# Gate/up blocks of a hybrid decoder layer: the first four pairs product by product on the unscaled residual stream

## The chip, the cores and the metric

The kernel runs on one core of a Trainium2 chip. The metric is the device time of one execution in microseconds (us). Weights and activations lie in device memory as float32 and reach the core's on-chip buffer by DMA; TensorE multiplies, its results land in PSUM banks of 512 float32 per partition, and VectorE, ScalarE and GpSimd do the rest.

## What is computed

One decoder block over 16 meta tokens and 512 tokens of width 1024: two token mixers (mLSTM and gated linear attention) side by side, then a SwiGLU channel mixer with 2816 hidden features and a final norm. The part that matters here, cut from the reference:

```python
def rmsnorm(x, g):
    y = xf * lax.rsqrt(jnp.mean(xf * xf, axis=-1, keepdims=True) + EPS)
    return (y * g.astype(jnp.float32)).astype(x.dtype)
...
    h = h + merged @ w_out[l].astype(dt)

    hn = rmsnorm(h, norm2_g[l])
    ff = jax.nn.silu(hn @ w_ff_gate[l].astype(dt)) * (hn @ w_ff_up[l].astype(dt))
    h = h + ff @ w_ff_down[l].astype(dt)

out = rmsnorm(h, final_g)
```

## The kernel before

Activations are kept transposed: features on the 128 partitions, the 512 tokens along a row. Each operand is split into a high part (a rounded copy, made by ScalarE) and a low part (the remainder, made by VectorE), and each product is three matmuls: high x high, high x low, low x high. For weights the copy is `whi` (line 215) and the remainder `wlo` (line 220); a unit of weights is 128x1024, loaded by SyncE into `raw` some units ahead.

Most products are done in pairs of feature blocks (`pair`, `seven`): the product of a 2x2 blocked operand by seven products of half the width instead of eight, called q1, q5, q6, p2, p3, p4 and p7. A pair has three PSUM banks (`bz`, `bx`, `by`). Some products add into the bank that an earlier one filled, after a copy of the earlier value has been taken out. A *sink* names what is done with the banks: copies s1, s7, s2 by ScalarE (lines 1641, 1642), additions c21, c11, c22 by VectorE (1643 to 1645), and `mid`, `c12`, `fin`. The weights of a pair are the gate and up rows, their sums (`wf`, line 254, and `wg`, line 266) and the splits of all of these; half of the sums come from DMAs that add to what is in the buffer.

In time the kernel goes through the projections, the two mixers, the branch products ("bm", "bg"), four pairs for the output projection ("out"), the feed-forward blocks, and the down product. The order in which an engine gets its work is the order in which the program writes it. Generators hold the side work; each product step advances them (`tick`), and `yield n` in one of them puts off its next piece by n steps. Tables (`PLAIN`, `FIRST`, `SECOND`, `DOWN`) say at which step of a unit the next units' weights are split.

After the out pairs, `residual` puts each block of h into `hres` and makes plain high and low operands `hf` of h times the norm's gain (lines 1494, 1495). The first four feature blocks (`NSTD`) are done plainly: `unit_real` (lines 335 to 337) does each gate and each up block as 8 x 3 matmuls of 512 columns on `hf`. Meanwhile `norm2` computes the row factor `rs2` (1 over the root mean square, one number per token), `operands` builds the seven operands for the pairs from h times gain times `rs2` (lines 1595 to 1616, splits 1586 and 1588), and `swiglu` multiplies gate and up by `rs2` (1552, 1553), takes Silu on ScalarE and forms their product on GpSimd (1557). The other 18 pairs follow: `sink_ff` applies Silu (line 144) and multiplies the halves (1637).

The down product goes through its seven products one after the other over all 11 pairs of hidden blocks; the results are added to `hres` (line 1740). Its last product, p3, is done output group by output group, 0, 1, 2, 3; groups 0 and 1 lie in one PSUM bank, 2 and 3 in another (`out_of`). Sums of down weights are formed ahead of time in device memory (`down_sums`, one step at each `next(sums)`) by GpSimd's and SyncE's DMA queues.

## Time and profile before

| | |
|---|---|
| median of 3 runs | 911.99 us (910.56 to 912.91) |
| profiled execution | 911.17 us |
| span in its trace | 909.4 us |
| TensorE busy | 894.3 us, 98% |
| VectorE / ScalarE / GpSimd busy | 707.0 / 582.5 / 129.0 us (78, 64, 14%) |
| out pairs, plain units | about 486 to 560 us, 560 to 606 us |
| 18 gate/up pairs, down product | 606 to 788 us, 788 to 900 us |

The span runs from the first to the last instruction that the profiler saw. Matmuls overlap in the records: one lasts longer than the time until the next one starts, so a pace is read from starts.

### The profile page before, as it was taken

What the parts mean: (1) busy time and instruction counts of PE and PEld (TensorE: products, weight loads), DVE (VectorE), ACT (ScalarE), POOL (GpSimd) and SP (SyncE); (2) the same over time, 40 slices, a digit from 0 to 9 for tenths busy, and PEclk for the clock granted to TensorE, in tenths of its full rate; (3) what the DMA queues carried; (4) which work ended last, traced back from release to release, by engine and by line L of the source; (5) the groups of instructions that cost most, each with busy time, mean ns of one, the idle gap of its engine ahead of it and who ended that gap; (6) DMA issues with size and microseconds to landing.
All of it is one profiled execution on the core that took longest, in us unless ns stands there. A gap on an engine that the chain in (4) does not pass through costs nothing. (4 is left out here: it accounts for less than half of the span.)

```text
span 909.4 us, 17138 instructions
## 1 busy us (share of the span) xinstructions
PE 894.3 (98%) x6615; PEld 852.4 (94%) x6615; DVE 707.0 (78%) x1144; ACT 582.5 (64%) x1062; POOL 129.0 (14%) x151
## 2 busy tenths in 40 slices
PE   9999999999999999999999999999999999999995
PEld 9998989899998899999997898879999999999995
DVE  4789676888865477787778988897767767889995
ACT  6578578898774275766774455645555555667673
POOL 0000022021211122222110112133112111000000
PEclk9999999999999999999999999999999999999998
DMA  9346274569885889888874788269777776475652
GB/s 339 135 159 181 84 188 89 144 185 243 208 221 171 213 227 246 218 210 187 175 166 128 191 223 209 70 157 207 182 202 173 191 202 155 116 221 175 192 146 93
DMA packets 73538, 164.22 MB, mean 181 GB/s; under 512 B 7184, under 2 KB 24720, under 8 KB 72112
## 3 DMA queue, kind: packets, MB, share of 16 engines
q1 hardware_dynamic: 50208, 125.20, 41.5%
q0 software_dynamic: 22016, 36.84, 26.1%
q10 hardware_dynamic: 1232, 1.09, 0.4%
q8 instruction: 51, 0.84, 0.4%
q14 instruction: 31, 0.25, 0.1%
HBM read 156.68 MB, written 28.44 MB: 204 GB/s over the span
## 5 line engine op out<-in xcount | busy, mean ns | idle before, releaser
L381 PE MATMUL b<-t,whi 128*128 128x256 f32 (+1 forms) x1008 | 288.8, 286 | 3.1 <-DVE t L1516 1.1
L383 PE MATMUL b<-t,wlo 128*128 128x256 f32 (+1 forms) x1008 | 284.4, 282 | 0.3 <-DVE wlo L220 0.3
L382 PE MATMUL b<-t,whi 128*128 128x256 f32 (+1 forms) x1008 | 284.6, 282 | 0.0
L220 DVE TENSOR_TENSOR wlo<-raw,whi 128x1024 fp32r<-128x1024 f32 (+2 forms) x175 | 209.1, 1196 | 91.0 <-ACT whi L215 90.7
L215 ACT CAST whi<-raw 128x1024 fp32r<-128x1024 f32 (+2 forms) x175 | 178.8, 1023 | 59.9 <-PE b L382 21.8
L381 PEld LDWEIGHTS b<-t,whi 128*128 128x128 f32 x1008 | 190.0, 188 | 4.8 <-DVE t L1516 1.5
L382 PEld LDWEIGHTS b<-t,whi 128*128 128x128 f32 x1008 | 190.1, 189 | 0.5
L383 PEld LDWEIGHTS b<-t,wlo 128*128 128x128 f32 x1008 | 189.9, 188 | 0.5 <-DVE wlo L220 0.5
L336 PE MATMUL b<-t,whi 128*128 128x264 f32 (+1 forms) x528 | 178.6, 338 | 0.2 <-DVE t L972 0.2
L335 PE MATMUL b<-t,whi 128*128 128x264 f32 (+1 forms) x480 | 162.2, 338 | 0.0
L337 PE MATMUL b<-t,wlo 128*128 128x264 f32 (+1 forms) x480 | 159.6, 332 | 0.0
L144 ACT ACTIVATE t<-t 128x512 f32<-128x512 f32 (+8 forms) x145 | 80.6, 573 | 53.2 <-DVE t L1316 22.8
L1793 PE MATMUL b<-t,whi 128*128 128x256 f32 x616 | 110.5, 282 | 1.0 <-DVE f L1740 1.0
L336 PEld LDWEIGHTS b<-t,whi 128*128 128x128 f32 x528 | 99.9, 189 | 11.8 <-DVE t L972 0.8
L335 PEld LDWEIGHTS b<-t,whi 128*128 128x128 f32 x480 | 91.1, 190 | 8.9 <-ACT t L967 0.3
L337 PEld LDWEIGHTS b<-t,wlo 128*128 128x128 f32 x480 | 90.8, 189 | 8.7
L1793 PEld LDWEIGHTS b<-t,whi 128*128 128x128 f32 x616 | 95.1, 189 | 1.4 <-DVE f L1740 1.4
L198 POOL DMA_DIRECT2D raw<-wst x42 | 37.0, 882 | 385.6 <-DMA raw<-wst 68.1
L1793 PE MATMUL b<-t,wlo 128*128 128x256 f32 x308 | 86.8, 282 | 0.0
L1793 PEld LDWEIGHTS b<-t,wlo 128*128 128x128 f32 x308 | 58.3, 189 | 0.0
L239 POOL DMA_DIRECT2D wf<-wst x42 | 41.3, 991 | 115.7 <-ACT t L144 33.4
L215 ACT CAST whi<-wf 128x1024 fp32r<-128x1024 f32 x42 | 44.0, 1048 | 19.9 <-PE b L382 11.6
(273 smaller groups left out, 1469.3 us busy)
## 6 DMA issues: line engine op xcount, KB each, us to landing
raw<-wst SPq DMA_DIRECT2D x131, 512.0 KB, 4.9
wf<-wst SPq DMA_DIRECT2D x42, 256.0 KB, 4.2
wf<-wst POOLq DMA_DIRECT2D x42, 256.0 KB, 6.4
raw<-wst POOLq DMA_DIRECT2D x42, 256.0 KB, 4.5
raw<-wdn SPq DMA_DIRECT2D x15, 512.0 KB, 3.7
sum_q<-wdn POOLq DMA_DIRECT2D x10, 512.0 KB, 9.3
raw<-sum_q SPq DMA_DIRECT2D x10, 512.0 KB, 3.6
sum_q<-wdn SPq DMA_DIRECT2D x5, 512.0 KB, 5.3
```

What stands on the lines that cost most here:

```text
L144: S.activation(o, i, func, **kw)
L198: G.dma_start(lr(r, 0), lr(wst[v - 1], 0), accum_op=ALU.add)
L215: S.copy(t, src)
L220: V.tensor_tensor(t, src, hi.bitcast(F32), ALU.subtract)
L239: G.dma_start(lr(st.f, 1), lr(wst[u + 1], 1), accum_op=ALU.add)
L335: T.matmul(o, w_h, ah[:, c0:c1], start=first, stop=False)
L336: T.matmul(o, w_h, al[:, c0:c1], start=False, stop=False)
L337: T.matmul(o, w_l, ah[:, c0:c1], start=False, stop=last)
L381: T.matmul(o, h, xh_[k][:, c0:c1], start=start and k == 0, stop=False, skip_group_check=not start)
L382: T.matmul(o, h, xl_[k][:, c0:c1], start=False, stop=False, skip_group_check=not start)
L383: T.matmul(o, l, xh_[k][:, c0:c1], start=False, stop=k == 3, skip_group_check=not start)
L1793: T.matmul(o, w[ws][:, j * P:(j + 1) * P], xd[n][k][:, xs_], start=fresh and step == 0, stop=step == 2 and k == FH - 1, skip_group_check=True)
```

## The change

The four plain blocks become one *group* of four gate and four up blocks that goes through the seven products one after the other, as the down product does: 14 chunks (`GCHUNKS`, 7 products by two halves of the inner dimension) of 24 matmuls with 256 columns. Their weights are sums formed ahead of time in device memory (`gsum`, from the new input `wgu`). The operands are h times gain without the row factor. They are built from `residual`'s copies during the out pairs, and `norm2` runs inside the group. Since gate and up would both need the row factor, only the gate is multiplied by it, ahead of Silu; the residual `hres` is divided by the factor once (the final norm doesn't see a factor of the row, but for its eps, which `done` adds in), so that ff and residual have the same scale. In `sink_ff` this puts a multiply (`gate`) ahead of each Silu. The product of `swiglu` on GpSimd is gone; VectorE does it in the group. Also: the groups of p3 run in the order 0, 2, 1, 3; the residual's loads (`load_x`) start in the "bg" units; one pair's weight sum is made by VectorE (`e_hi`); some `yield` numbers differ.

```diff
+LAST = (0, 2, 1, 3)
+GCHUNKS = [(n, k) for n in ORDER for k in (0, 2)]
 CHUNKS = [(n, 0, k, min(2, FH - k)) for n in ORDER[:-1] for k in range(0, FH, 2)] + [
-    ("p3", i, k, n) for i in range(4) for k, n in ((0, 6), (6, 5))]
+    ("p3", i, k, n) for i in LAST for k, n in ((0, 6), (6, 5))]
...
     def e_hi(u):
+        if u == FF0:
+            r = lr(raws[u + 1], 0)
+            V.tensor_tensor(r, r, lr(raws[u], 0), ALU.add)
         mixw[u].eh = whi(raws[u + 1])
...
-        if what in ("bm", "bg") and i % 2 or len(job) == 2:
+        if what in ("bm", "bg") and i % 2 or len(job) == 2 or job in JOBS[3:8]:
             next(sums, None)
...
-            if i == 3:
-                load_x(0)
+            if i in (1, 2, 5, 6):
+                load_x(2 * (1, 5, 2, 6).index(i))
...
     def residual(m, t):
         hres.append(t)
-        g = pr[:, C_N2 + m:C_N2 + m + 1]
-        a, b = tt(F32R, NS), tt(F32R, NS)
-        act(a, t, AF.Copy, scale=g)
-        V.scalar_tensor_tensor(b, t, g, a.bitcast(F32), ALU.mult, ALU.subtract)
-        hf[0].append(a)
-        hf[1].append(b)
...
+        act(hx[m // 2][:, m % 2], t, AF.Copy, scale=pr[:, C_N2 + m:C_N2 + m + 1])
+        full[0] = m + 1
+        yield 3
+        yield from add_square(m, t)
...
+        V.scalar_tensor_tensor(r, x, -2.0, y, ALU.mult, ALU.mult)
+        nbank.v = None
+        yield 42
+        for m in range(8):
+            yield 9
+            V.tensor_tensor(hres[m], hres[m], r, ALU.mult)
...
-        t1, t2 = tt(n=NS), tt(n=NS)
-        V.tensor_tensor(t1, og, rs2.v, ALU.mult)
-        V.scalar_tensor_tensor(t2, ou, -1.0, rs2.v, ALU.mult, ALU.mult)
-        yield 2
-        act(t1, t1, AF.Silu)
-        yield 5
-        G.tensor_tensor(t2, t1, t2, ALU.mult)
...
+            def gate(c, src):
+                V.tensor_tensor(g[:, c], src, rs2.v[:, c], ALU.mult)
+                act(g[:, c], g[:, c], AF.Silu)
...
-                mid=lambda: act(g[:, lo], g[:, lo], AF.Silu), c12=lambda: act(g[:, hi], bx, AF.Silu), fin=fin)
+                mid=lambda: gate(lo, g[:, lo]), c12=lambda: gate(hi, bx), fin=fin)
...
-    for m in range(NSTD):
-        og = unit_real(("fg", m), hf[0], hf[1])
...
-        ou = unit_real(("fu", m), hf[0], hf[1])
-        run(swiglu(m, og, ou))
...
+        then = dict(q1=lambda: copies(gx.s1, at["q1"]), q5=lambda: copies(gx.s5, at["q5"]),
+                    p2=lambda: silu(gx.g, at["p2"], gx.s1, slice(0, HS)), p7=lambda: copies(gx.s7, at["p7"]), q6=after_q6,
+                    p4=lambda: added(gx.c, at["p4"], gx.s2[:]), p3=done)
+        for c, (n, k0) in enumerate(GCHUNKS):
+            u, steps = begin(("fx", c))
+            w = splits.pop(u)
+            if c % 2 == 0:
+                next(sums, None)
+                at[n] = at[INTO[n]] if n in INTO else [bank(), bank()]
+            for j in range(8):
+                k, i = k0 + j // 4, j % 4
+                while n not in xw or len(xw[n][1]) <= k:
+                    tick()
...
+                T.matmul(o, h, xh_, start=fresh, stop=False, skip_group_check=True)
+                T.matmul(o, h, xl_, start=False, stop=False, skip_group_check=True)
+                T.matmul(o, l, xh_, start=False, stop=k == 3, skip_group_check=True)
...
+            if k0:
+                run(then[n]())
...
-            for i in range(4):
+            for i in LAST:
                 for k in range(FH):
```

How the instructions stand on three of the engines, before and with the change (line numbers are each kernel's own; in square brackets what an instruction waits for).

TensorE in p3 of the down product, where one output group ends and the next begins; `b_...` is a PSUM bank, `t_...` the activations, `whi_...` and `wlo_...` the weights. Before:

```order
L1793 MATMUL b_9727<-t_10823,whi_10773 128x256 x2
L1793 MATMUL b_9727<-t_10823,wlo_10791 128x256
L1793 MATMUL b_9727<-t_10619,whi_10815 128x256 x2
L1793 MATMUL b_9727<-t_10619,wlo_10828 128x256
L1793 MATMUL b_9727<-t_10637,whi_10815 128x256 x2
L1793 MATMUL b_9727<-t_10637,wlo_10828 128x256
```

With the change:

```order
L1885 MATMUL b_9962<-t_11060,whi_11010 128x256 x2
L1885 MATMUL b_9962<-t_11060,wlo_11028 128x256
L1885 MATMUL b_9963<-t_10855,whi_11052 128x256 x2
L1885 MATMUL b_9963<-t_10855,wlo_11065 128x256
L1885 MATMUL b_9963<-t_10873,whi_11052 128x256 x2
L1885 MATMUL b_9963<-t_10873,wlo_11065 128x256
```

The second group lay in the bank of the first, and lies in the other bank now; its half of that other bank is written while the first half of it waits to be taken out.

VectorE in the last stretch ahead of the first gate/up pair and into it: before, the remainders of the pairs' weights (`wlo_7213` of the first pair, `wlo_7224` of the second) between operands of line 1588 and the plain blocks' multiplies.

```order
L266 TENSOR_TENSOR wg_7158<-wf_6529,raw_6934 128x512
L1588 TENSOR_TENSOR t_7160<-t_7086,t_7151 128x512 [waits Activation_49]
L1588 TENSOR_TENSOR t_7170<-hx_6774,t_7153 128x512 [waits Activation_49]
L1552 TENSOR_TENSOR t_7190<-b_7065,t_6878 128x512 [waits PE_49]
L1553 SCALAR_TENSOR_TENSOR t_7191<-b_7119,t_6878 128x512 [waits PE_49]
L220 TENSOR_TENSOR wlo_7213<-wf_6529,whi_7147 128x1024 [waits DMASW3_49]
L1588 TENSOR_TENSOR t_7218<-hx_6774,t_7162 128x512 [waits Activation_49]
L220 TENSOR_TENSOR wlo_7224<-raw_7066,whi_7222 128x1024 [waits DMAHW4_49,DMASW2_49,Activation_49]
L254 TENSOR_TENSOR wf_6668<-raw_7066 128x512
L285 TENSOR_TENSOR wgl_7249<-wg_7158,wgh_7232 128x512 [waits DVE_49,Activation_49]
```

With the change, the same place: line 1689 adds the group's results, line 1708 forms its products, line 261 is the weight sum of the first pair, and `wlo_7310` and `wlo_7346` are the remainders of its weights.

```order
L261 TENSOR_TENSOR raw_7218<-raw_7218,raw_7185 128x512 [waits DMAHW1_49,DMAHW0_49]
L1689 TENSOR_TENSOR t_7300<-t_7183,t_7021 128x512
L1689 TENSOR_TENSOR t_7302<-b_7063,t_7229 128x512 [waits PE_49,Activation_49]
L233 TENSOR_TENSOR wlo_7310<-raw_7218,whi_7298 128x1024 [waits Activation_49]
L270 TENSOR_TENSOR wf_6543<-raw_7218 128x512
L1708 TENSOR_TENSOR t_7276<-t_7276,t_7229 128x512
L1689 TENSOR_TENSOR t_7321<-b_7064,t_7252 128x512 [waits PE_49]
L1708 TENSOR_TENSOR t_7300<-t_7300,t_7252 128x512 [waits DVE_49]
L233 TENSOR_TENSOR wlo_7346<-raw_7185,whi_7338 128x1024 [waits Activation_49]
L282 TENSOR_TENSOR wg_7356<-wf_6543,raw_7185 128x512 [waits DVE_49]
L1689 TENSOR_TENSOR t_7380<-b_6893,t_7229 128x512 [waits PE_49]
L1689 TENSOR_TENSOR t_7394<-b_6894,t_7252 128x512 [waits PE_49]
```

The operands have left this place for the out pairs; the group's sums, with waits for TensorE, stand in it now, between the remainders.

VectorE in one gate/up pair in the middle of the stretch, before:

```order
L220 TENSOR_TENSOR wlo_8122<-raw_7936,whi_8111 128x1024 [waits DMASW2_49,DMAHW2_49,PE_49,Activation_49]
L1637 TENSOR_TENSOR t_7944<-t_7944,t_7945 128x512 [waits DVE_49,Activation_49]
L254 TENSOR_TENSOR wf_7963<-raw_7936 128x512
L285 TENSOR_TENSOR wgl_8148<-wg_8057,wgh_8131 128x512 [waits PE_49,Activation_49]
L1643 TENSOR_TENSOR t_8072<-b_8067,t_8071 128x256 [waits PE_49,Activation_49]
L220 TENSOR_TENSOR wlo_8168<-raw_7934,whi_8159 128x1024 [waits DMAHW1_49,Activation_49]
L1644 TENSOR_TENSOR t_8073<-b_8069,t_8070 128x256 [waits PE_49]
L266 TENSOR_TENSOR wg_8185<-wf_7963,raw_7934 128x512 [waits DVE_49]
L1645 TENSOR_TENSOR t_8072<-t_8070,t_8071 128x256 [waits Activation_49]
```

With the change (line 233 is `wlo`, line 1656 `fin`, line 1660 the multiply by the row factor):

```order
L233 TENSOR_TENSOR wlo_8984<-raw_8795,whi_8973 128x1024 [waits DMASW3_49,DMAHW7_49,PE_49,Activation_49]
L1660 TENSOR_TENSOR t_8804<-b_8799,t_7175 128x256 [waits PE_49]
L1656 TENSOR_TENSOR t_8803<-t_8803,t_8804 128x512 [waits Activation_49]
L270 TENSOR_TENSOR wf_8823<-raw_8795 128x512
L302 TENSOR_TENSOR wgl_9011<-wg_8918,wgh_8994 128x512 [waits Activation_49]
L1666 TENSOR_TENSOR t_8933<-b_8928,t_8932 128x256 [waits PE_49,Activation_49]
L233 TENSOR_TENSOR wlo_9031<-raw_8793,whi_9022 128x1024 [waits DMAHW6_49,Activation_49]
L1667 TENSOR_TENSOR t_8934<-b_8930,t_8931 128x256 [waits PE_49]
L282 TENSOR_TENSOR wg_9048<-wf_8823,raw_8793 128x512 [waits DVE_49]
L1660 TENSOR_TENSOR t_8934<-t_8934,t_7175 128x256 [waits DVE_49]
L1668 TENSOR_TENSOR t_8933<-t_8931,t_8932 128x256 [waits Activation_49]
```

Two multiplies of line 1660 have come in, one straight behind the first remainder, on the bank `b_8799` itself, and one behind c11 (before line 1644, now 1667).

## Rows read from the trace of the kernel before

**Rows 1.** The page's busy time of TensorE (time, share of the span, instructions), and from its strip of 40 slices the granted clock of TensorE in tenths and the busy share of the DMA engines in tenths.

```profile
PE 894.3 (98%) x6615; PEld 852.4 (94%) x6615; DVE 707.0 (78%) x1144; ACT 582.5 (64%) x1062; POOL 129.0 (14%) x151
...
PEclk9999999999999999999999999999999999999998
DMA  9346274569885889888874788269777776475652
```

**Rows 2.** The busy time of each engine (with its instructions in brackets), the granted clock, the DMA share and rate in four stretches: the last out pairs, the eight plain units, the down product, and the 18 gate/up pairs.

```profile
525.00:566.00 41.00, 39.87 (x313) 38.15 (x311) 34.35 (x57) 23.47 (x35) 7.55 (x9) 1.00 0.83 207
567.00:610.00 43.00, 42.33 (x196) 34.89 (x195) 40.22 (x55) 22.71 (x31) 9.65 (x6) 1.00 0.44 116
...
800.00:880.00 80.00, 80.00 (x675) 80.00 (x674) 74.73 (x158) 53.35 (x103) 0.00 (x0) 1.00 0.62 182
...
611.00:790.00 179.00, 178.77 (x1514) 178.77 (x1515) 131.01 (x191) 103.50 (x191) 31.97 (x35) 1.00 0.71 179
```

**Rows 3.** TensorE's timeline at both ends of the plain units: start, duration, engine, line, operation. Line 335 to 337 are the 512-column matmuls of the plain units, line 381 to 383 the 256-column ones of pairs.

```profile
560.28 0.40 PE L336 MATMUL b<-t,whi 128*128 128x512 f32 x1
...
562.13 0.28 PE L381 MATMUL b<-t,wgh 128*128 128x256 f32 x1
...
565.61 0.40 PE L335 MATMUL b<-t,whi 128*128 128x512 f32 x1
566.01 0.50 PE L336 MATMUL b<-t,whi 128*128 128x512 f32 x1
...
606.34 0.28 PE L381 MATMUL b<-t,whi 128*128 128x256 f32 x1
```

**Rows 4.** What TensorE waited for from the out pairs to the first gate/up pair (486 to 612 us), and from there into the down product (612 to 905 us): engine, its line, what it waited for; us in total, times, the longest.

```profile
PE b L381 <- DVE t L1516: 1.1, 2, 1.0
PE b L381 <- ACT t L1641: 1.1, 1, 1.1
PE b L383 <- DVE wlo L220: 0.3, 1, 0.3
...
PE b L1793 <- DVE f L1740: 1.0, 2, 0.5
```

**Rows 5.** The timelines of VectorE and TensorE around the longest wait of an out pair. In brackets: idle time before, and its releaser.

```profile
546.75 1.41 DVE L1495 SCALAR_TENSOR_TENSOR t<-f,pr,t 128x512 fp32r<-128x512 f32 x2 [0.20 <-ACT t L144]
548.08 0.42 DVE L1516 TENSOR_TENSOR t<-b,t 128x256 f32<-128x256 f32 x1
548.41 0.68 DVE L285 TENSOR_TENSOR wgl<-wg,wgh 128x512 fp32r<-128x512 f32 x1
...
548.55 0.38 PE L381 MATMUL b<-t,whi 128*128 128x256 f32 x1 [0.98 <-DVE t L1516]
```

**Rows 6.** The timelines of ScalarE and TensorE around the wait at the start of the first gate/up pair.

```profile
609.48 0.63 ACT L144 ACTIVATE t<-t 128x512 f32<-128x512 f32 x1 [1.35 <-DVE t L1552]
610.02 0.63 ACT L1641 COPY t<-b 128x256 f32<-128x256 f32 x2
...
610.42 0.39 PE L381 MATMUL b<-t,whi 128*128 128x256 f32 x1 [1.09 <-ACT t L1641]
```

**Rows 7.** The timelines of VectorE and TensorE around the two waits between the four p3 groups of the down product.

```profile
884.52 0.96 DVE L220 TENSOR_TENSOR wlo<-raw,whi 128x768 fp32r<-128x768 f32 x1
885.50 0.75 DVE L1740 TENSOR_TENSOR f<-f,b 128x256 f32<-128x256 f32 x2
...
885.97 0.51 PE L1793 MATMUL b<-t,whi 128*128 128x256 f32 x2 [0.52 <-DVE f L1740]
...
895.05 0.51 PE L1793 MATMUL b<-t,whi 128*128 128x256 f32 x2 [0.51 <-DVE f L1740]
```

**Rows 8.** The timelines of VectorE and GpSimd in the plain units, beside the longest product on GpSimd (line 1557).

```profile
601.11 0.68 DVE L1606 TENSOR_TENSOR t<-hx,hx 128x512 f32<-128x512 f32 x1
601.71 0.68 DVE L1588 TENSOR_TENSOR t<-t,t 128x512 fp32r<-128x512 f32 x1
602.43 1.67 DVE L1611 TENSOR_TENSOR t<-t,hx 128x512 f32<-128x512 f32 x1
...
599.78 3.77 POOL L1557 TENSOR_TENSOR t<-t,t 128x512 f32<-128x512 f32 x1
```

**Rows 9.** The timelines of ScalarE, VectorE and TensorE at the change from one gate/up pair to the next, in the middle of the pairs.

```profile
641.12 0.40 ACT L144 ACTIVATE t<-b 128x256 f32<-128x256 f32 x1
641.39 0.64 ACT L280 CAST wgh<-wg 128x512 fp32r<-128x512 f32 x1
642.46 0.37 ACT L1641 COPY t<-b 128x256 f32<-128x256 f32 x1 [0.43 <-PE b L383]
...
641.26 1.23 DVE L220 TENSOR_TENSOR wlo<-raw,whi 128x1024 fp32r<-128x1024 f32 x1 [2.50 <-ACT whi L215]
642.40 0.68 DVE L1637 TENSOR_TENSOR t<-t,t 128x512 f32<-128x512 f32 x1
...
640.84 0.28 PE L381 MATMUL b<-t,whi 128*128 128x256 f32 x1
```

**Rows 10.** ScalarE's timeline around the table load of the norm.

```profile
570.50 1.28 ACT L143 ACT_TABLE_LOAD   x1
571.80 0.69 ACT L144 ACTIVATE t<-b,cb 128x512 f32<-128x512 f32 x1
```

More of the change, by code (lines that the diff above doesn't have):

```diff
@@ L76, in job_list @@
     for m in range(FT):
-        o += one(("fg", m), ("fu", m)) if m < NSTD else [(("fg", m), ("fu", m))]
+        if m == 0:
+            for i in range(len(GCHUNKS)):
+                o += one(("fx", i))
+        if m >= NG:
+            o += [(("fg", m), ("fu", m))]
     for i in range(len(CHUNKS)):
@@ L92 @@
 DN0 = UNITS.index(("down", 0))
+ROW = {u: i for i, u in enumerate(u for u in range(NUNITS) if UNITS[u][0] not in ("fx", "down"))}
 MIXED = [UNITS.index(j[0]) for j in JOBS if len(j) == 2]
+LAST_OUT = UNITS.index(("out", 6))
+FF0 = UNITS.index(("fg", NG))
 ITEMS = [i for j in JOBS for i in ([("s", UNITS.index(j[0]))] if len(j) == 1 else
@@ new lines, in operands, with high, low, both @@
+    def operands():
+        three = lambda a: a.rearrange("p (j n) -> p j n", j=2)
+        L, R = slice(0, HS), slice(HS, NS)
+        def high(n, i, c):
+            src = hx[i][:, :, c]
+            hi = tt(F32R, NS)
+            S.copy(three(hi), src)
+            xw[n][0].extend(three(hi)[:, j] for j in range(2))
+            return n, src, hi
+        def low(n, src, hi):
+            lo = tt(F32R, NS)
+            V.tensor_tensor(three(lo), src, three(hi).bitcast(F32), ALU.subtract)
+            xw[n][1].extend(three(lo)[:, j] for j in range(2))
+        def both(n, i, c):
+            a = high(n, i, c)
+            yield 1
+            low(*a)
+        for n in SEVEN:
+            xw[n] = [], []
+        for i in (0, 1):
+            while full[0] < 2 * i + 2:
+                yield 2
+            yield 2
+            t = hx[i]
+            yield from both("q1", i, L)
+            yield 3
+            V.tensor_tensor(t[:, :, L], t[:, :, L], t[:, :, R], ALU.subtract)
+            yield 1
+            yield from both("q5", i, L)
+        for i in (2, 3):
+            while full[0] < 2 * i + 2:
+                yield 6
+            yield 1
+            yield from both("p2", i, L)
+            yield 1
+            t, b = hx[i - 2], hx[i]
+            V.tensor_tensor(t[:, :, R], b[:, :, R], t[:, :, R], ALU.subtract)
+            yield 2
+            yield from both("p7", i - 2, R)
+        for i in (0, 1):
+            t, b = hx[i], hx[i + 2]
+            V.scalar_tensor_tensor(t[:, :, L], t[:, :, L], -1.0, b[:, :, R], ALU.mult, ALU.subtract)
+            yield 1
+            yield from both("q6", i, L)
+        for i in (0, 1):
+            t, b = hx[i], hx[i + 2]
+            V.scalar_tensor_tensor(b[:, :, L], t[:, :, L], -1.0, b[:, :, L], ALU.mult, ALU.subtract)
+            yield 5
+            yield from both("p4", i + 2, L)
+        for i in (2, 3):
+            yield 1
+            yield from both("p3", i, R)
@@ L1522, in sink_out @@
         return sink
+    run(operands())
     for i in range(4):
         pair((("out", 2 * i), ("out", 2 * i + 1)), mg, (0, 256), sink_out(2 * i), i == 0)
-    while len(hf[1]) < 6:
-        tick()
-    rs2 = box()
-    def norm2():
-        yield 1
-        sh, sl = tt(F32R, NS), tt(F32R, NS)
-        S.copy(sh, acc[0])
-        V.tensor_tensor(sl, acc[0], sh.bitcast(F32), ALU.subtract)
-        yield 3
-        ps = bank()
-        T.matmul(ps, onesr, sh, start=True, stop=False)
-        T.matmul(ps, onesr, sl, start=False, stop=True)
-        yield 3
-        rs2.v = rsqrt_mean([(ps, 0, NS)], float(D), NS)
-        acc.clear()
@@ L1630, in sink_ff @@
+    nbank = box()
+    nbank.v = bank()
+    ff = [None] * FT
     def sink_ff(m):
@@ L1836, in hybrid_block @@
                         make_op(nxt, k, 1)
-                if x == 0 and k == 0:
-                    left("p3", "c12", "fin")
+                if x == 0 and k < 2:
+                    left(*(("p3", "c12") if k == 0 else ("fin",)))
                 xd[n][k] = None
```

288 lines of the change are left out of this document (155 added, 133 removed).

## Prediction

> **What bounds the kernel now.** I began with the page's busy times and the strip of 40 slices [rows 1]: TensorE is busy 98% of the span and its granted clock stands at 9 tenths in all but the last slice, so the end is set by how many columns it multiplies and by the few places where it stands still; VectorE, ScalarE and GpSimd matter only there. Next the stretches that the change touches, out pairs, plain blocks, pairs, down product [rows 2]: in all four PE is busy for nearly the whole stretch; VectorE (DVE) is at 40.22 of 43.00 us in the plain blocks, at 131.01 of 179.00 in the pairs. Then the timeline of PE at both ends of the plain blocks [rows 3], since records of neighbouring matmuls overlap and only starts tell a pace. Last PE's waits [rows 4] and, around the longest of them, the other engines' timelines [rows 5 to 7].
>
> **PE's own work.** Eight plain units are 8 x 24 = 192 matmuls of 512 columns. From the first of them that [rows 3] shows to the pair after them is 606.34 - 560.28 = 46.06 us; in it lie 12 narrow matmuls of the pair that was left over (1.42 us at the narrow pace below), two wide ones of the norm (0.46) and a short wait (0.40 from start to start at 565.61 in place of 0.23, and 0.1 more behind it: 0.27); 43.9 us are left, 0.229 each. The group in their place does 14 chunks x 24 = 336 matmuls of 256 columns (7 products of 4 blocks instead of 8, at half the width). The pairs run 1514 narrow ones in 179.00 us and the down product 675 in 80.00 [rows 2]: 0.1182 and 0.1185 each, so 336 take 39.8 us. With rounding of either pace I take -4.3 us; all else that PE multiplies stays.
>
> The Trainium skill would have it the other way: its "TensorE: Matmul & The Clock Gate", section Back-to-back issue gap, gives a sustained 131 ns for 512 columns and 81 ns for 128. By an estimate between these two (98 ns for 256) the change would cost 336 x 0.098 - 192 x 0.131 = +7.7 us. The trace doesn't agree: 0.229 and 0.118 are in the ratio of the widths, and the measurement decides; it gets no chance below.
>
> **The stalls that go.** What a stall costs is more than the idle time that its row prints: a record lasts 0.28 where the next starts 0.12 later, and the first matmul after a stall is 0.1 longer; idle + 0.26 us.
> - Out pairs, before PE line 381 [rows 4, 5]: 0.98 idle at 548.55, so 1.24 us. The first product's matmuls wait for DVE's add (line 1516), which stands behind two splits of line 1495 (1.41 us). The change drops these splits (they were the plain units' operands), and the operand parts that take their place are issued later in the pair, behind that add. The other of the two waits of that row (1.1 less 1.0 idle, so some 0.4) comes in the first out pair, before any split, and stays. The operands' work is now spread over these pairs, and DVE is at 34.35 of 41.00 us there [rows 2]; I leave 0.35 us for late evacuations. Out: -1.24 + 0.35 = -0.9.
> - Down product [rows 4, 7]: groups of output 1 and 3 wait, 0.52 and 0.51 idle, for the evacuation (line 1740) of the group that PE has just ended, 0.78 us each. Both groups lie in one PSUM bank. With the order 0, 2, 1, 3 PE goes on in the other bank, and 3.9 us pass before it comes back. The next weights' low half (line 220, 884.52 + 0.96) ends at about the moment when PE, not stopped, would come to it, so I take -1.3 of -1.56.
>
> **DVE in the group, the term that may go wrong.** In the stretch of 42 us DVE now has 13 low halves of 1024, 36 operations of 512 and 4 of 256. By the pace from start to start (1.14 in [rows 9]; 0.60 in [rows 8]; 0.33 in [rows 5]) that is 14.8 + 21.6 + 1.3 = 37.7 us, against 350 matmuls x 0.1185 = 41.5 us of PE: 91%. Late in it is tight: from the start of product p4 to the first pair's third matmul PE has 98 matmuls, 11.6 us, and DVE 4 x 1.14 + 14 x 0.60 = 13.0 us. So the first pair waits about 1.5 us for the low half of its own weights; the first pair then has, by the order, 10.6 us of DVE for 9.95 of PE (84 matmuls), another 0.3; from the next on 8.7 of 9.95 while the residual is divided (8 operations), 7.5 after that. Before, the first pair lost 1.35 + 0.56 = 1.9 us: Silu stood behind line 1552 of DVE, the copy of line 1641 behind Silu, and then the low half [rows 4, 6]. That chain is gone; its successor is the low half alone.
> ScalarE's chain in the group, from the norm's matmuls: two casts, the norm's table change (1.28 us), two functions and the copies of product p7 [rows 10], 6.1 us in all; the second copy ends about when p4 begins to write that bank. I price it at 0.2. So here -1.9 + 1.5 + 0.3 + 0.2 = +0.1, between -1.9 (DVE keeps up) and +3.5: with the recorded durations (1.22, 0.68, 0.42) in place of the paces DVE needs 42.1 us of 41.5.
> The Trainium skill ("ScalarE: Activation LUTs", What ACT_TABLE_LOAD costs) adds a drain of 1380 ns to each load of 1283 ns; that would put +0.7 on this term. The trace shows the load of 1.28 us and the next function 0.02 us after its end [rows 10], so I don't.
>
> **The pairs.** Each of 18 gets two more operations on DVE (line 1660, the row factor on the gate) and its Silu waits for them. DVE has room: 73% and 0.33 x 2 more of 9.95. What counts is the chain at the end of a pair [rows 9]: q6 starts at 640.84 and product q5 must have its bank free 36 matmuls later, at 645.1. Now the copy for that ends at 642.46 + 0.37. With the change: low half to 642.40, gate multiply to 642.75, Silu to 643.15, cast of 0.64 and copy of 0.37, ended by 644.1 to 644.2. 0.9 us are left, so nothing.
>
> **GpSimd.** Its product goes (3.77 us at worst [rows 8]), and with it what it did to DVE: the operation beside it took 1.67 us where its neighbour of that shape took 0.68. That gain lies in the plain blocks, where DVE has no stall left but those above; it is contained in them.
>
> **Edits at nothing.** Eight more sums through DRAM are issued early, in slices 2 to 5, whose DMA share is 2 to 7 tenths [rows 1]; the residual's loads move to the bg units, whose slices (20 and 21, counted from 0) stand at 7 and 4. PE waits for no DMA in the rows shown [rows 4]; the price if this cover fails is about a microsecond for one late weight. The final norm's extra operation is off the path.
>
> **Sum.** 911.17 (the profiled execution: span 909.4 and 1.8 around it) - 4.3 - 0.9 - 1.3 + 0.1 = 904.8. The median of the three runs is 0.8 above that execution: 905.6.
>
> **Rivals.**
> - DVE becomes the bound of the group: recorded durations, not paces, hold, and the first pairs start 3.5 us late. For it: 91% in a stretch where order and waits are fixed; against: the paces are measured where DVE had a queue. 905.6 + 3.4 = 909.0. Chance 0.20.
> - Slower than before: the gate's multiply delays each pair. If DVE comes to it over 0.9 us later than read above (one low half more in front of it is enough, 1.14), Silu and the copy miss the start of q5 by some 0.7 us in every pair: 18 x 0.7 = 12.6, 918. Against: the order has only the one low half in front. Chance 0.06.
> - All of it goes: the out pairs keep no rest, the first pair waits less than 0.5: 905.6 - 2.5 = 903.1. Chance 0.17.
> - It doesn't do what it says at the end: PE still waits there, for low halves in place of banks: 905.6 + 1.3 = 906.9. Chance 0.12.
> - My forecast, 904.3 to 906.5: chance 0.45.
>
> **Numbers.** A measurement of this kernel tells about 0.3% (2.7 us) from no change: faster means below 909.3, slower above 914.7. Forecast, all-of-it and no-change-at-the-end are faster (0.74), with them some half of the first rival (0.10): 0.84. Same takes the rest of that rival: 0.10. Slower 0.06. The range runs from 902.0, past the favourable case, to 909.5, past the first rival; outside lie the pairs' rival and part of the first one, under 2 in 10.
>
> **What would show it.** PE's 256-column rows of the group at 0.118 from start to start with no wait but DVE's low half near its end; no wait for DVE's f at the end; line 1495 and its wait gone from out pairs; DVE over 0.9 busy in the group; no PE wait in the pairs from the second on. It is wrong if the first pair waits over 3 us, if waits for ScalarE's copy come in every pair, or if DMA appears among PE's releasers.

## The result and the profile after

The changed kernel takes 905.28 us (median of four, 904.59 to 906.02) where the kernel before takes 912.42: ratio 0.9926, 95% interval 0.9908 to 0.9943. Taken once more, later, it was 0.9924 (0.9909 to 0.9938). In microseconds of a kernel of 912 that is -6.8 (-5.2 to -8.4 by the interval); the forecast was -6.4 (905.6), its range 902.0 to 909.5. Where a run is said below to be so many us over the changed kernel, that is the difference of the two ratios (the changed kernel's at 0.9924 to 0.9926), times 912.

The total came out, but not by the terms it was summed from. The page of the changed kernel, the lines that answer to [rows 1]:

```profile
PE 891.9 (99%) x6759; PEld 858.6 (95%) x6759; DVE 721.5 (80%) x1192; ACT 592.6 (66%) x1076; POOL 126.1 (14%) x154
...
PEclk9999999999999999999999999999999999999998
DMA  9875364778986789888867767987776776466552
```

TensorE (PE) has 144 matmul records more, 336 narrow ones for 192 wide ones, and is busy 2.4 us less. VectorE (DVE) went from 707.0 to 721.5 us with 48 operations more, 36 of them the two multiplies in each pair.

The stretches that answer to [rows 2]: out pairs, group, pairs, down product.

```profile
525.00:560.00 35.00, 34.66 (x285) 33.93 (x285) 31.59 (x54) 24.10 (x36) 6.53 (x7) 1.00 0.77 179
560.00:602.00 42.00, 42.00 (x353) 41.92 (x352) 39.60 (x55) 32.21 (x44) 9.86 (x9) 1.00 0.92 245
...
606.00:786.00 180.00, 179.69 (x1513) 179.48 (x1513) 146.94 (x236) 104.34 (x191) 27.99 (x32) 1.00 0.67 177
795.00:875.00 80.00, 80.00 (x673) 80.00 (x673) 75.69 (x159) 54.34 (x104) 0.00 (x0) 1.00 0.62 185
```

In the group VectorE is busy 39.60 of 42.00 us (94%), and the DMA share is 0.92 where the plain units had 0.44: seven products read 14 chunks of weights, and the sums for the down product run beside them. Yet PE is busy in all of it. What PE waited for from the out pairs to the end, to be read against [rows 4]:

```profile
PE b L1859 <- ACT t L154: 0.5, 1, 0.5
PE b L400 <- DVE wlo L233: 0.3, 1, 0.3
```

Five waits are gone: both for line 1516, the one for ScalarE's copy at the first pair, both for line 1740 in the down product. The wait for the final norm stays (line 1767 before, 0.5 as well), and one of 0.3 us for a low half, now in the second pair.

Stages are best compared by the start of their first matmul: that of the out pairs (at about 520 us, so the 486 of the table ahead is too early for them), of the group or the plain units, of the first gate/up pair, the matmul 1500 further on, and PE's last end. The table has the time from each to the next, for both kernels and for runs of the experiments that have the same stages:

| us from stage start to stage start | (start of the out pairs) | out pairs | plain units / group | 1500 matmuls of pairs | down product |
|---|---|---|---|---|---|
| before | 519.68 | 40.37 | 46.29 | 178.95 | 115.27 |
| before, p3 order alone changed | 520.95 | 39.25 | 46.36 | 179.51 | 113.71 |
| before, products on VectorE alone | 520.49 | 39.12 | 46.70 | 178.09 | 115.26 |
| before, both of these | 520.88 | 39.16 | 47.67 | 178.06 | 113.73 |
| changed | 520.88 | 39.95 | 41.97 | 178.78 | 113.79 |
| changed, again | 519.89 | 39.95 | 41.98 | 178.21 | 113.79 |
| changed, p3 in the old order | 519.63 | 39.93 | 41.98 | 178.53 | 115.29 |

Two columns repeat the forecast: the group (-4.3) and the down product (-1.5). Two don't: the out pairs, where the profile of before is an outlier of its own kernel, and the pairs, which hardly moved although the first one lost most of its 1.9 us of waits. The first column is no effect of the change. The first matmuls start 0.22 us apart, later ones 0.12; that changes at 9.3 us in the profile of before and at 11.8 us in that of the changed kernel, but at 9.8 us in its second profile, and it is where these profiles' starts part.

One difference lies outside the stages. Of 65 executions of the kernel before that were timed beside the experiments, 21 had a mean granted clock of 0.994 or 0.995 and took 913.4 us on average; the other 44 had 0.996 or 0.997 and took 911.7. The changed kernel had 0.996 or more in all ten of its executions. So about 0.5 us of the 6.8 (21 of 65 times 1.7, an estimate) goes with a lower clock that the kernel before has in a third of its executions; the profile of before (911.17, 0.997) is not one of these. Where in the kernel before the clock falls is not known, since no such execution of it was profiled. In four of the experiments below an execution with such a fall was profiled, and there it comes at a long stop of PE.

### The profile page after: what moved, and what is told of

It is laid out like the page before. It is cut to its first block, busy times and chain, and to the rows that moved or that the text cites. A ratio compares the mean times of both kernels' runs of the same rounds, so it can differ in the third digit from the quotient of the medians.

```text
span 904.2 us, 17474 instructions
## 1 busy us (share of the span) xinstructions
PE 891.9 (99%) x6759; PEld 858.6 (95%) x6759; DVE 721.5 (80%) x1192; ACT 592.6 (66%) x1076; POOL 126.1 (14%) x154
## 3 DMA queue, kind: packets, MB, share of 16 engines
q10 hardware_dynamic: 1232, 1.09, 0.4%
## 5 line engine op out<-in xcount | busy, mean ns | idle before, releaser
L233 DVE TENSOR_TENSOR wlo<-raw,whi 128x1024 fp32r<-128x1024 f32 (+2 forms) x181 | 214.7, 1188 | 65.8 <-ACT whi L228 65.0
L228 ACT CAST whi<-raw 128x1024 fp32r<-128x1024 f32 (+2 forms) x181 | 185.1, 1024 | 38.3 <-PE b L353 9.9
L398 PEld LDWEIGHTS b<-t,whi 128*128 128x128 f32 x1008 | 190.2, 189 | 2.8 <-ACT t L482 0.6
L399 PEld LDWEIGHTS b<-t,whi 128*128 128x128 f32 x1008 | 190.4, 189 | 0.4
L400 PEld LDWEIGHTS b<-t,wlo 128*128 128x128 f32 x1008 | 190.0, 188 | 0.5 <-DVE wlo L233 0.5
L353 PE MATMUL b<-t,whi 128*128 128x264 f32 (+1 forms) x464 | 153.9, 332 | 0.4 <-DVE t L989 0.2
L154 ACT ACTIVATE t<-t 128x512 f32<-128x512 f32 (+8 forms) x161 | 86.7, 555 | 88.8 <-DVE t L1660 46.9
L352 PE MATMUL b<-t,whi 128*128 128x264 f32 (+1 forms) x416 | 137.6, 331 | 0.0
L354 PE MATMUL b<-t,wlo 128*128 128x264 f32 (+1 forms) x416 | 135.0, 325 | 0.0
L353 PEld LDWEIGHTS b<-t,whi 128*128 128x128 f32 x464 | 88.3, 190 | 9.1 <-DVE t L989 0.8
L1885 PEld LDWEIGHTS b<-t,whi 128*128 128x128 f32 x616 | 95.2, 190 | 0.0
L352 PEld LDWEIGHTS b<-t,whi 128*128 128x128 f32 x416 | 79.5, 191 | 6.2 <-ACT t L984 0.2
L354 PEld LDWEIGHTS b<-t,wlo 128*128 128x128 f32 x416 | 79.4, 191 | 6.2
L1885 PEld LDWEIGHTS b<-t,wlo 128*128 128x128 f32 x308 | 58.4, 190 | 0.0
```

The lines of the kernel that those rows point to most:

```text
L154: S.activation(o, i, func, **kw)
L228: S.copy(t, src)
L233: V.tensor_tensor(t, src, hi.bitcast(F32), ALU.subtract)
L352: T.matmul(o, w_h, ah[:, c0:c1], start=first, stop=False)
L353: T.matmul(o, w_h, al[:, c0:c1], start=False, stop=False)
L354: T.matmul(o, w_l, ah[:, c0:c1], start=False, stop=last)
```

## The experiments

### The order of the last four groups, alone and taken back

```diff
-    ("p3", i, k, n) for i in range(4) for k, n in ((0, 6), (6, 5))]
+    ("p3", i, k, n) for i in LAST for k, n in ((0, 6), (6, 5))]
```

with the loop over the groups alike: put into the kernel before (first), and `LAST = (0, 1, 2, 3)` in the changed one (second).

> The kernel before with one part of the change alone: the four groups of p3 in the order 0, 2, 1, 3. Theory (each of the two waits is for the bank of the group just ended, 0.78 us each with the restart): both waits for line 1740 disappear, time 1.3 to 1.6 us under the kernel before. Rival (PE then waits for the next weights' low half instead): a wait for the low half of some 0.5 us appears at the same two places, gain under 0.6 us.

> The changed kernel with the four groups of p3 in the old order 0, 1, 2, 3. Theory: the two waits for the evacuation come back at 0.5 idle each, time 1.3 to 1.6 us over the changed kernel (about 906.8 on a chip where that makes 905.3). Rival: another thing in the changed kernel had removed the waits, then nothing changes.

Into the kernel before: 0.9993 (0.9980 to 1.0005), so -0.6 us with an interval from -1.8 to +0.5. Its trace:

```profile
PE b L382 <- ACT t L1642: 1.7, 1, 1.7
PE b L1768 <- ACT t L145: 0.5, 1, 0.5
PE b L384 <- DVE wlo L221: 0.3, 1, 0.3
PE b L382 <- DVE t L1517: 0.2, 1, 0.2
```

No wait for line 1741 (1740 before) is left, none for a low half took its place, and the down product is 1.56 us shorter in the table. But this execution's first pair waits 1.7 us for the copy where [rows 6] shows 1.09: that wait differs by more than half a microsecond between two executions with the same order up to there. Taken out of the changed kernel, both waits are back at 0.51 idle each (down product 1.50 longer), ratio 0.9942 (0.9930 to 0.9954), 1.6 us over the changed kernel. By the traces the theory holds, both ways; the time of the first run falls short of the 1.3 to 1.6 us expected and would not have shown it.

### GpSimd's product

```diff
-        G.tensor_tensor(t2, t1, t2, ALU.mult)
+        V.tensor_tensor(t2, t1, t2, ALU.mult)
```

in the kernel before; and in the changed kernel the reverse, its four products of the group's end on GpSimd:

```diff
-                V.tensor_tensor(gx.c[j], gx.c[j], gx.g[j], ALU.mult)
+                G.tensor_tensor(gx.c[j], gx.c[j], gx.g[j], ALU.mult)
...
-                V.tensor_tensor(gx.d[j], gx.d[j], gx.h[j], ALU.mult)
+                G.tensor_tensor(gx.d[j], gx.d[j], gx.h[j], ALU.mult)
```

> The kernel before with the four products of gate and up of the plain blocks on VectorE in place of GpSimd: VectorE gets 4 x 0.60 = 2.4 us and is rid of the stretched operations (three of them about 1.1 us each over their neighbours). Theory of the prediction (contained in the waits at the first pair, which VectorE's lateness sets): 0 to 1.5 us faster than the kernel before, by a shorter wait for the copy behind Silu at the first pair. Rival (VectorE's queue is the longer for it): the first pair's wait grows, 0.5 to 2 us slower.

> The changed kernel with the four products of gate and up at the group's end on GpSimd in place of VectorE, as the kernel before had its own. VectorE is rid of 4 x 0.60 = 2.4 us. Theory (GpSimd's product holds VectorE up by about 1.0 us each where they meet, as 1.67 against 0.68 showed): VectorE is 1.6 us or more worse off, and as it has 0.2 us to spare at the first pair's third matmul and the first products lie ahead of that, the first pair starts to wait: 0.5 to 2.5 us slower. Rival (nothing hangs on it, the two engines hardly meet): within 0.4 us of the changed kernel, VectorE's operations beside it at 0.68.

The kernel before gains from having the product on VectorE: 0.9973 (0.9963 to 0.9983), -2.5 us. PE's waits there:

```profile
PE b L1793 <- DVE f L1740: 1.0, 2, 0.5
PE b L1767 <- ACT t L144: 0.5, 1, 0.5
PE b L383 <- DVE wlo L220: 0.3, 1, 0.3
PE b L381 <- ACT t L1641: 0.2, 1, 0.2
PE b L1540 <- DVE t L1536: 0.2, 1, 0.2
```

The copy's wait at the first pair fell from 1.09 (1.66 in the profile above) to 0.23, though VectorE has four operations more; the norm's second matmul now waits 0.18. The gain is above the 0 to 1.5 us that the theory gave. The other way round it costs more than I had said: 0.9968 (0.9958 to 0.9978), 4.0 us over the changed kernel. VectorE and GpSimd at the first pair of that kernel:

```profile
609.15 2.68 DVE L1699 TENSOR_TENSOR t<-t,t 128x512 f32<-128x512 f32 x1
611.76 0.68 DVE L302 TENSOR_TENSOR wgl<-wg,wgh 128x512 fp32r<-128x512 f32 x1
...
613.46 1.23 DVE L233 TENSOR_TENSOR wlo<-raw,whi 128x1024 fp32r<-128x1024 f32 x1 [0.70 <-ACT whi L228]
...
609.39 1.89 POOL L1714 TENSOR_TENSOR t<-t,t 128x512 f32<-128x512 f32 x1
...
PE b L400 <- DVE wlo L233: 1.9, 3, 0.8
PE b L398 <- ACT whi L228: 1.2, 1, 1.2
```

The gate multiply that took 0.68 us everywhere else takes 2.68 beside GpSimd's product of 1.89; Silu, the next cast and the low half follow it, and PE waits twice. The other three products do the same further on: a weight sum of line 270 takes 3.51 (from 621.50) beside two products of 1.64 and 1.61, an operation of line 1560 takes 2.22 (from 634.16) beside one of 1.61, and PE waits for a low half in each of those pairs: four waits, 3.1 us idle in all. Behind the first two of them (1.19 and 0.76 us) the granted clock is 0.50 from 614.8 to 618.2 us, 1.2 GHz in place of 2.4. That comes in some executions only: the two of ten with a mean clock of 0.994, the profiled one among them, took 910.4 and 910.8 us, the others 907.3 to 909.1.

Both parts together in the kernel before:

> The kernel before with two parts of the change and without its group: the p3 groups in the order 0, 2, 1, 3, and the plain blocks' products on VectorE. Alone they gave 0.9993 and 0.9973 of the time before. Theory (they are separate waits, so they add): -1.5 by the trace's two waits and -2.1 to -2.5 by the earlier first pair, 908 to 908.8 where before makes 912. Theory that a third wait takes over: above 909.5. It is also a further look at the out pairs as they were before: the 0.98 us wait for line 1516 that the profile of before shows at 548 was in neither of two other executions with the same out pairs; if it is chance, it stays away here too, if it belongs to that program's timing, it may come.

0.9962 (0.9949 to 0.9974), -3.5 us: they add, about. So of the change's 6.8 us some 3.5 (2.4 to 4.7 by the interval) are to be had without the group. In this profile a new wait eats a part of the gain: the norm's two matmuls wait 0.6 and 0.2 us, and the plain units take 47.67 us. And this third profile of the old out pairs has no long wait for line 1516 either.

### How late VectorE is at the group's end

The group's last 24 matmuls are left out:

```diff
-                T.matmul(o, h, xh_, start=fresh, stop=False, skip_group_check=True)
...
+                if c < len(GCHUNKS) - 1:
+                    T.matmul(o, h, xh_, start=fresh, stop=False, skip_group_check=True)
...
```

> The changed kernel without the 24 matmuls of the group's last chunk (half of product p3 of the first four blocks is left out of the result); its weights are still loaded and split, and all else stays. PE has 24 x 0.119 = 2.9 us less to do. Theory that VectorE is as late as it can be at the group's end (the low half that the first pair's third matmul reads was ready 0.2 us ahead of it): the first pair waits for that low half by 2.4 to 2.7 us, and the time falls by 0.2 to 0.8 us only. Rival (PE alone sets the pace, VectorE's order leaves room): 2.5 to 2.9 us faster than the changed kernel.

0.9925 (0.9904 to 0.9947): nothing is gained on the whole by 2.9 us less of PE's work. First the end of the group in the changed kernel, then in this one:

```profile
601.10 0.68 DVE L1708 TENSOR_TENSOR t<-t,t 128x512 f32<-128x512 f32 x1
601.70 1.22 DVE L233 TENSOR_TENSOR wlo<-raw,whi 128x1024 fp32r<-128x1024 f32 x1
602.83 0.68 DVE L282 TENSOR_TENSOR wg<-wf,raw 128x512 f32<-128x512 f32 x1
...
602.80 0.28 PE L398 MATMUL b<-t,whi 128*128 128x256 f32 x1
...
603.04 0.31 PE L400 MATMUL b<-t,wlo 128*128 128x256 f32 x1
```

```profile
601.38 0.68 DVE L1708 TENSOR_TENSOR t<-t,t 128x512 f32<-128x512 f32 x1
601.97 1.22 DVE L233 TENSOR_TENSOR wlo<-raw,whi 128x1024 fp32r<-128x1024 f32 x1
603.11 0.68 DVE L282 TENSOR_TENSOR wg<-wf,raw 128x512 f32<-128x512 f32 x1
...
600.23 0.28 PE L398 MATMUL b<-t,whi 128*128 128x256 f32 x1
...
603.25 0.58 PE L400 MATMUL b<-t,wlo 128*128 128x256 f32 x1 [2.62 <-DVE wlo L233]
```

In the changed kernel the low half that begins at 601.70 gives way to the next operation at 602.83, and the third matmul of the first pair reads it at 603.04, without a wait. With 24 matmuls fewer the pair begins at 600.23, the low half is no earlier, and PE stands still for 2.62 us. VectorE bounds the group's end as much as PE does; the group can't be made shorter on PE alone.

The stop costs more than its 2.62 us in this execution. The granted clock behind it, against the stretch after that:

```profile
603.30:606.20 2.90, 2.90 (x14) 2.90 (x15) 2.90 (x5) 0.37 (x1) 0.00 (x0) 0.50 1.10 263
606.40:609.40 3.00, 3.00 (x27) 3.00 (x27) 0.89 (x2) 1.92 (x4) 0.00 (x0) 1.00 0.60 231
```

Until 606.2 the clock is at the lower of its two levels, 1.2 GHz, and matmuls start 0.21 us apart. So the time says less than the wait does: two of the four executions have a mean clock of 0.992 and 0.995 and took 907.7 and 907.0 us; the two with 0.997 took 904.1 and 904.6, some 0.8 under the changed kernel, the gain of 0.2 to 0.8 that was expected.

### The slack of the gate multiply

The multiply on the bank, ahead of the pair's second Silu, executed three and five times (no value changes):

```diff
-                V.tensor_tensor(g[:, c], src, rs2.v[:, c], ALU.mult)
+                for _ in range(5 if c.start else 1):
+                    V.tensor_tensor(g[:, c], src, rs2.v[:, c], ALU.mult)
```

> The changed kernel with the second gate multiply of each pair (on the bank, ahead of the Silu whose successor copy must be done before product q5) executed three times in place of once, which changes no value and adds 0.66 us ahead of that Silu. Theory of the prediction (some 0.9 to 1.1 us are left between the copy's end and the start of q5): hidden, within 0.7 us of the changed kernel, no new wait in the pairs. Rival (the slack is smaller, or VectorE at 0.8 busy can't take more): a wait in most pairs, 18 x 0.3 = 5 us and more.

> The same with five in place of one, 1.32 us ahead of the Silu. Theory: 0.2 to 0.4 us past the slack and 0.1 for the restart, so a wait for the copy before q5 in nearly every pair, 18 x 0.3 to 0.5 = 5 to 9 us over the changed kernel. Rival (the chain doesn't set that start): within 0.7 us.

Two more: 0.9948 (0.9932 to 0.9965), 2.1 us over the changed kernel, where the theory had at most 0.7 and no wait; three pairs wait, 0.23 to 0.63 us idle. Four more: 1.0105 (1.0085 to 1.0126), 16 us over it, where 5 to 9 were expected, and 17 waits:

```profile
PE b L398 <- ACT t L1665: 12.2, 17, 1.2
```

```profile
727.46 2.25 DVE L1661 TENSOR_TENSOR t<-b,t 128x256 f32<-128x256 f32 x5
...
718.89 0.42 ACT L154 ACTIVATE t<-t 128x256 f32<-128x256 f32 x1 [3.46 <-DVE t L1661]
719.22 0.60 ACT L297 CAST wgh<-wg 128x512 fp32r<-128x512 f32 x1
719.73 0.36 ACT L1665 COPY t<-b 128x256 f32<-128x256 f32 x1
...
720.14 0.39 PE L398 MATMUL b<-t,whi 128*128 128x256 f32 x1 [0.63 <-ACT t L1665]
```

(Lines from 1660 on have a number one higher in this kernel: 1661 is the multiply, 1665 the copy that was 1664.) The chain is the predicted one: multiplies, Silu, cast, copy, and q5 at 720.14 waits for the copy. Its size fits the predicted one once the dose is read right: repeated multiplies into the same tile follow each other by 0.46 us, not 0.33 (five take 2.25 in place of 0.42), so four more add 1.83. PE is late by 0.80 and loses 0.1 at the restart; 1.83 - 0.80 leaves 1.03 us of slack, where 0.9 had been read off the trace of before. Two more add 0.9, which uses the slack up: it holds in most pairs and not in three.

### The sums that run beside the group

```diff
             if c % 2 == 0:
-                next(sums, None)
...
     for m in range(NG, FT):
         next(sums, None)
+        if NG < m <= NG + 7:
+            next(sums, None)
```

> The changed kernel with the seven steps of weight sums that it issues in the group moved into pairs 2 to 8 (two steps each there). The one wait left at the first pairs (low half, 0.48 us, at 613.6) goes back by the chain to a weight's added half that took 6.75 us to land against a median of 4.6, at a DMA share of 0.9. Theory that the sums' traffic makes it late: it lands within 5 us and the wait is gone, 0.4 to 0.6 us faster. Rival (the transfers of the weights themselves fill the DMA engines there, or the buffer is freed late by VectorE): it still lands after 6 us and more, the wait stays, no change within 0.3 us.

0.9993 (0.9983 to 1.0003): 6.3 us over the changed kernel, which neither theory had. The group's DMA share falls to 0.68 and the wait for the low half at the first pairs isn't there, but

```profile
PE b L398 <- ACT t L1664: 5.7, 2, 4.8
```

```profile
632.19 1.25 POOL L1243 DMA_DIRECT2D s<-wdn  x1 [7.04 <-issue]
632.94 1.42 POOL L211 DMA_DIRECT2D raw<-wst  x1
...
641.26 1.04 ACT L228 CAST whi<-raw 128x1024 fp32r<-128x1024 f32 x1 [5.82 <-issue]
```

PE waits 4.8 us in the fifth pair (and 0.9 in the third). GpSimd's DMA queue works in order here: the sum's accumulating DMA (line 1243) comes up at 625.1 and starts only at 632.19, 0.36 us after the accumulating DMA before it has landed (631.83), and one that completes a weight (line 211) stands behind it. Issued at 632.94, that one lands at 641.20, and ScalarE's cast of this weight starts at 641.26, 5.8 us after its last work. In the changed kernel the same issue comes at 629.27 and lands at 633.87. So the weight is 7.3 us later, half of it by its place behind the sum, half because it takes 8.3 us to land in place of 4.6 beside the sums' traffic. In this execution the granted clock is 0.50 from 645.2 to 651 us as well, behind the long stop; it took 913.4 us where the median is 911.09. Left beside the group, the seven steps of sums lead to no wait but perhaps the short one in the second pair; moved into the pairs they cost 6 us.

The wait that this was to explain is seen in one profile of the changed kernel (0.32 idle at 613.6; 0.48 with the slower restart), as 0.07 in the one with the old p3 order, and not at all in a further one (below). An edit that puts the second gate multiply of the group's end ahead of the low half that waits for the late weight:

```diff
                 V.tensor_tensor(v, v, rs2.v[:, c].unsqueeze(1).to_broadcast([P, 2, HS]), ALU.mult)
-                yield 2
+            yield 1
+            for j in range(2):
                 act(o[j], o[j], AF.Silu)
                 yield 1
```

> The changed kernel with the group's last two gate multiplies straight one behind the other (the second had stood behind a low half and a weight sum that wait for a late DMA), and the two Silu behind them. Theory (the chain late weight, low half, second multiply, Silu, cast, low half makes the 0.48 us wait at the first pairs): the wait goes, 0.3 to 0.6 us faster than the changed kernel. Rival (the cast waits for its own weight as well): the wait stays, within 0.3 us.

> The changed kernel once more, unaltered, for a second profile and more times. Theory (its gain is 0.7 to 0.75% and the last experiment's version is 0.4 to 0.6 us better by one wait): ratio to the kernel before 0.992 to 0.993, and a wait for the low half at the first pairs again, 0.1 to 0.5 us. Rival (the last experiment changed nothing, its 0.9915 is chance): ratio 0.991 to 0.992 here as well, and no such wait in this profile either. In both the four short waits of the out pairs, 0.1 us idle each, stand as before and the start differs by up to 1.3 us between executions.

The version with the early multiply: 0.9915 (0.9901 to 0.9928), 905.28 us beside 912.83. The changed kernel again: 0.9924, and PE's waits in it are

```profile
PE b L1859 <- ACT t L154: 0.5, 1, 0.5
```

so the wait comes in some executions only. The rival, that the edit changed nothing, can't be ruled out: 0.8 us between the two versions lies inside both intervals, and that the early multiply helps isn't shown.

### The pace of the pairs

> The changed kernel with a buffer pool of 59 slots in place of 60: every engine's instructions in the same order, 637 of 676 temporary tiles at other addresses. In the pairs matmuls start 118.7 ns apart on average in every execution of the changed kernel and 118.0 in every one of the kernel before, position by position alike from pair to pair. Theory that the addresses of the operands do it: the pattern by position changes and the average moves by some tenths of a ns (1500 matmuls: up to 1 us either way). Rival (the work beside it does, two more VectorE operations for each pair): the pattern and 118.7 stay.

```diff
-NTT = 60
+NTT = 59
```

Counts of matmuls in the same 120 us inside the pairs, in the kernel before, the changed one and this one:

```profile
650.00:770.00 120.00, 120.00 (x1019) 120.00 (x1019) 85.00 (x120) 67.72 (x123) 20.98 (x24) 1.00 0.74 190
```

```profile
650.00:770.00 120.00, 120.00 (x1013) 120.00 (x1012) 95.26 (x150) 67.39 (x121) 19.55 (x23) 1.00 0.71 183
```

```profile
650.00:770.00 120.00, 120.00 (x1015) 120.00 (x1015) 95.34 (x150) 67.51 (x121) 21.02 (x24) 1.00 0.72 183
```

1019, 1013 and 1015 matmuls: 0.1178, 0.1185 and 0.1182 us each; from start to start over 13 pairs, without the matmuls that stick out of the window, 0.1180, 0.1187 and 0.1184. The same count came back in a second profile of either kernel (1019 and 1013), and by position in a pair the start-to-start time of each matmul is a fixed number between 0.112 and 0.125. With every engine's instructions in the same order and only the temporary tiles elsewhere, the pattern and the average moved. So the addresses matter; by which rule isn't known. The move is 0.3 ns of the 0.7 ns that lie between the kernel before and the changed one: whether placement makes up all of these, or VectorE's additional operations have a part, isn't shown. For 1500 matmuls the changed kernel's pace costs 1.0 us against before. As a whole this kernel was 0.9943 (0.9929 to 0.9956), slower than the changed one, but not in the pairs: with one slot fewer PE waits 2.1 us early on, for ScalarE at line 481, where it waited 0.5 in the changed kernel, and behind that stop the granted clock is 0.50 from 201.5 to 204.9 us.

## Why the prediction came out, step by step

- **PE's own work, -4.3: right.** 46.29 became 41.97. The prediction's two numbers give 39.8 - 43.9 = -4.1, which it rounded up; the plain stage's short wait, 0.27, is in the measured difference besides. 512 columns at 0.229 and 256 at 0.118 were what the trace had said; the group ran at 0.119. By the sustained gaps that the Trainium skill gives ("TensorE: Matmul & The Clock Gate", Back-to-back issue gap) the stage would have grown by 7.7, by the prediction's estimate; the trace doesn't agree, they don't hold for these matmuls.
- **The end of the down product, -1.3: right, and whole.** 115.27 to 113.79, -1.5. The low half that I feared would come late caused no wait.
- **Out pairs, -0.9: wrong in sign against typical executions.** The step that failed is "1.24 us at 548.55 goes with the splits of line 1495": the wait belonged to that one execution. The same out pairs, run three more times, took 39.12 to 39.25 us in place of 40.37. The changed ones take 39.9 to 40.0 in every run with the same placement. Besides the short stops of the first two pairs, which were there before, the third and the fourth now stop as well, where a product needs a bank that VectorE has yet to empty (line 1632). In the third:

```profile
543.53 0.68 DVE L1576 TENSOR_TENSOR t<-hx,t 128x512 fp32r<-128x512 f32 x1
544.13 0.42 DVE L1632 TENSOR_TENSOR t<-b,t 128x256 f32<-128x256 f32 x1
...
544.30 0.28 PE L400 MATMUL b<-t,wgl 128*128 128x256 f32 x1
544.70 0.36 PE L398 MATMUL b<-t,whi 128*128 128x256 f32 x1
```

Starts 0.40 apart (0.38 in the fourth, at 555.04) where 0.12 is the pace. Ahead of line 1632 on VectorE stands the low part of one of the group's operands (line 1576): it is the work that the change moved here. I had left 0.35 us for such late evacuations; with what the restarts lose these two are 0.7, and the stage is 0.7 to 0.8 over what it typically took.
- **VectorE in the group, "the first pair waits about 1.5 us": wrong by its size; the mechanism was right.** The third matmul had its low half 0.2 us early. I counted 14 operations of 512 between p4's start and that low half; the timeline has 11, as VectorE, which was not late up to there, had done the norm's three before p4 began. That is 1.8 us, and turns 1.5 late into about 0.2 early. The term of +0.1 should have been -1.3 to -1.9: the waits of 1.9 went, and what came in their place was a wait of 0.6 with its restart, or none. That nothing more is left was shown by the run with fewer matmuls. The ScalarE term (0.2 at p4) is nil.
- **The pairs, nothing, by a slack of 0.9: right.** Measured 1.03, in most pairs.
- **GpSimd, "contained": wrong.** Alone, in the kernel before, it is worth -2.5 us by the times, of which the table shows about 1 in the pairs' column. I had let a new wait of the first pair eat the gain; it didn't come.
- **Edits at nothing: no loss was found where they are**, but not because the DMA engines have room. The prediction priced a late weight at about a microsecond, with no row behind it; moved into the pairs, where a weight stands behind them in GpSimd's queue, seven steps of sums cost 6.
- **Not in the sum at all:** +1.0 us in the pairs by the pace, and about -0.5 by the lower clock that the kernel before has in a third of its executions.

So the total came out by luck: the out pairs were 1.7 us worse than their term, the first pairs 1.4 to 2.0 better than theirs, and a pace and a clock that no term had pull in opposite directions.

By the table, stage by stage and against typical executions: out +0.8, group -4.3, pairs -0.2 to -1.3 (waits of the first pair gone, 1.0 given back by the pace), down product -1.5: -5.2 to -6.3. Added up within one execution each, the four stages are 380.9 us before and 380.4 with the p3 order alone changed (its 1.5 put back), 374.5 and 373.9 in the changed kernel: -5.9 to -6.9. With the 0.5 us of the lower clock that covers the 6.8 that the times say. These are two profiles a side, and the waits of the kernel before come and go, so how the rest falls on single terms stays open by about half a microsecond.

## What to carry to other kernels

A wait seen in one profile may be that execution's own: before a term is built on it, see whether what sets it (a late DMA, an engine a few tenths behind) has a reason to come back. Where two engines are both above 0.9 busy in a stage, taking work from one alone gained next to nothing here; count what the other still has to do from the same instant, and subtract what it has done by then. An operation that costs nothing in one stage's queue can hold up a weight in another's, and the order of that DMA queue is what to read there. And the time of a run that makes PE stop can hold more than the stop: the granted clock behind it belongs beside the waits.

## What was not expected of the hardware

- The start-to-start time of 256-column matmuls is fixed position by position (0.112 to 0.125 us) and moves with the addresses of tiles: averages over the pairs of 0.1187 and 0.1184 us for two placements of the same instructions, 0.1180 in the kernel before.
- Behind a stop of PE of 2.62 us (the group's end with fewer matmuls), of 4.78 us (sums in the pairs), of 2.06 us (one slot fewer) and of 1.19 and 0.76 us 1.3 us apart (products on GpSimd) the granted clock was 0.50, 1.2 GHz, in the stretch that followed, and matmuls of 256 columns started 0.21 us apart in place of 0.12. Behind the 17 stops of 0.6 to 1.2 us with four more multiplies and the one of 1.66 us with the p3 order alone it stayed at 1.00.
- A VectorE multiply of 0.68 us took 2.68 beside a GpSimd product of 1.89: 2.0 us were added, about that product's whole duration. The other stretched operations give 2.8 us beside 3.25 and 1.5 beside 1.61. The Trainium skill ("SBUF — State Buffer", Who interferes with whom) has a VectorE operation with two inputs in SBUF and a GpSimd operation that reads SBUF exclude each other, the second to issue being held up. The trace agrees with the size; but here the one that by the record started first (609.15 against 609.39) was held up. A GpSimd record's start is rough, so the order is not settled.
- Repeated VectorE operations of 256 elements into one tile follow each other by 0.46 us (five take 2.25), independent ones by 0.33.
